# Scores of two attention groups: two products over stacked copies, or three products of 64 rows each

## The chip, the cores and the metric

The kernel runs on one core of a Trainium2 chip. The metric is the device time of one execution in microseconds (us): median 1858.41 us of three runs (1857.59 to 1861.31). The engines are named as in the profile: PE (matrix products), PEld (the loading of a product's stationary operand, which runs beside PE), DVE, ACT, POOL, SP (issues the DMAs).

## The reference

Two layers of a transformer trunk over 512 latent and 256 context tokens of width 1024. The input projection of each layer feeds four head groups in parallel: A (windowed attention, 4 query heads on 2 key heads, with a sink), B (differential attention), C (retention), D (2-D neighbourhood attention, 4 heads). Their outputs go through one output projection, then an MLP. The change touches the scores of A and D alone, per query block of 128 tokens:

```python
# A, per head
s_win  = einsum('bgrnqd,bgnkd->bgrnqk', qb, kw) * scale      # up to 3 key blocks of 128
s_win  = where(valid, s_win, NEG_INF)
s_ctx  = einsum('bgrnqd,bgkd->bgrnqk', qb, k_ctx) * scale    # 256 context keys
prob   = softmax_f32(concatenate([s_win, s_ctx, s_sink], -1))
# D, per head
s      = einsum('bhrjqd,bhrjkwd->bhrjqkw', qg, kg) * scale + bias
s_ctx  = einsum('bhrjqd,bhkd->bhrjqk', qg, k_ctx) * scale
prob   = softmax_f32(concatenate([where(col_valid, s, NEG_INF), s_ctx], -1))
```

A head has 64 channels. Everything is float32; the result of the second layer for the latent tokens is the output.

## The kernel before

Activations lie transposed, channels on the 128 partitions and tokens along the free dimension. Products run on float32r operands, and where float32 accuracy is wanted a value is split into a high part and a low part (`split`): a projection (`gemm`, lines 314 to 328) makes three products per weight tile, high by high (L321), high by low (L322), low by high (L326).

One tile of queries or keys holds two heads of 64 channels, one in partitions 0 to 63 and one in 64 to 127. For A, B, C and D the kernel makes stacked copies of it. `qstack` (L605) makes one tile per head with the high part of that head in one half of the partitions and its low part in the other. `kstack` (L614) makes two tiles per head, one with the high part in both halves and one with the low part in both; the second half is filled by a DMA from the first (`KCOPY`). `qkmm` (L702) then needs two products over all 128 rows for a head: queries by high keys and queries by low keys, which together are all four partial products.

`band_pair` (L737) takes two (block, head) items: in A the two query heads that share a key head, in D two query blocks of one head. The context scores of both items (128 x 256 each) go to the two halves of one PSUM tile `psc`; the window scores of each (128 x 256 at the first and last block, 128 x 384 at the two between, none for context queries) go to a PSUM tile of their own. The tag `ps` has two buffers (`PSB = 2`). DVE adds mask or bias and takes the row maximum while it copies the scores to SBUF (L735, L757), ACT takes the exponential (L763) and scales (L770); then PE transposes the probabilities (L809 in A, L1025 in D) and multiplies by the values (`pvmm`, L713 to L716). The products at L713 and L716 have 64 columns of weights.

`weave` (L106) writes the program: the attention of one unit is mixed with the projections of the next units, by the costs that the generators yield and the totals `CA0` to `CD1`. A scheduler then sets the order on each engine from priorities, readiness and buffers; on PE that order is fixed. `rstd`, `meansq` and `mod_mm` make float32 products with 32 columns of weights, three or four side by side in different column quarters of the array (L244, L266, L350); they are called quarter products below.

Of the kernel before, what the change touches and what calls it, by code (L numbers as in the profile page):

```python
# [12 lines left out]
OP = mybir.AluOpType  # L13
# [5 lines left out]
NT = NX + NC_  # L19
# [3 lines left out]
NEG = -1e30  # L23
# [131 lines left out]
def body(ctx: ExitStack, tc, A):  # L155
    nc = tc.nc
    V, S, G, T, SY = nc.vector, nc.scalar, nc.gpsimd, nc.tensor, nc.sync
# [19 lines left out]
    def pso():  # L177
        return pp.tile([128, 512], F32, name=nm("po"), tag="po", bufs=POB)

    def pss():  # L180
        return pp.tile([128, 512], F32, name=nm("ps"), tag="ps", bufs=PSB)
# [7 lines left out]
    for w in (128, 64, 32):  # L189
        t = cons.tile([128, 32], F32, name=f"gmean{w}")  # L190
# [7 lines left out]
    with tc.tile_pool(name="sp0", bufs=1) as sp0:  # L198
        t = sp0.tile([128, 3, 128], F32, name="spread0")
        V.memset(t, 0.0)  # L200
        for j in range(3):
            r = slice(32 * j, 32 * j + 32)
# [75 lines left out]
    def split(src, hi, lo):  # L278
        S.activation(hi, src, AF.Copy)  # L279
        V.tensor_tensor(lo, src, hi.bitcast(F32), op=OP.subtract)  # L280
# [52 lines left out]
    def u3r(p):  # L333
        return main.tile([128, 768], F32R, name=nm(p), tag="u3", bufs=U3)
# [138 lines left out]
    for L in range(DEPTH):  # L473
        last = L == DEPTH - 1
        nq = NX if last else NT
        lam_init = 0.8 - 0.6 * math.exp(-0.3 * L)
        cl = colc[:, L, :]
        rb = rowb[:, L, :]
# [5 lines left out]
        if L == 0:  # L484
# [38 lines left out]
            h = htiles()  # L523
# [24 lines left out]
        else:  # L548
            xsrc = xd
            h = hnext  # L550
# [6 lines left out]
        GI = {}  # L557
# [26 lines left out]
        def oft(c):  # L584
            of[c] = u3("of")
            return of[c]
# [16 lines left out]
        HALF = (slice(0, 64), slice(64, 128))  # L603
# [10 lines left out]
        def kstack(t, n):  # L614
# [7 lines left out]
                KCOPY(y[b, :n], y[a, :n])  # L622
            return st, lo

        def quarter(i):
            return slice(32 * i, 32 * i + 32)

# [74 lines left out]
        def qkmm(o, q, k, h, qs, ks, keys_first):  # L702

            for i, part in enumerate(k):
                x, y = q[h][:, qs], part[h][:, ks]
                if keys_first:
                    x, y = y, x
                T.matmul(o, lhsT=x, rhs=y, start=(i == 0), stop=(i == 1))

        def pvmm(po, c0, l, vv, hh, t, ph, pl, start, stop):  # L710

            if stop:
                T.matmul(po[0:64, c0:c0 + l], lhsT=vv[:, hh, t, 0:64], rhs=pl, start=False, stop=False)  # L713
            T.matmul(po[:, c0:c0 + l], lhsT=vv[:, hh, t], rhs=ph, start=start, stop=stop)  # L714
            if not stop:
                T.matmul(po[0:64, c0:c0 + l], lhsT=vv[:, hh, t, 0:64], rhs=pl, start=False, stop=False)  # L716
# [16 lines left out]
        def rowmax(dst, src, init, acc):  # L733

            V.tensor_tensor_reduce(dst, src, zcol.to_broadcast([128, src.shape[-1]]), 1.0, init, OP.add, OP.max, acc)  # L735

        def band_pair(items, sinks):  # L737


            sm = smalls()  # L740
            psc = pss()
            res = []
            for i, (n, q, k, h, mask) in enumerate(items):
                qs = slice(128 * n, 128 * n + 128)
                qkmm(psc[:, 256 * i:256 * i + 256], q, k, h, qs, slice(512, 768), False)
            yield 700
            for i, (n, q, k, h, mask) in enumerate(items):
                win = [] if n >= 4 else [t for t in (n - 1, n, n + 1) if 0 <= t < 4]
                w = 128 * len(win)
                P = ptile()  # L750
                rowmax(P[:, w:w + 256], psc[:, 256 * i:256 * i + 256], NEG if sinks is None else sinks[:, i:i + 1], sm[:, i:i + 1])
                if w:
                    qs = slice(128 * n, 128 * n + 128)
                    ks = slice(128 * win[0], 128 * win[0] + w)
                    ps = pss()
                    qkmm(ps[:, :w], q, k, h, qs, ks, False)
                    V.tensor_tensor_reduce(P[:, :w], ps[:, :w], mask, 1.0, sm[:, i:i + 1], OP.add, OP.max, sm[:, 2 + i:3 + i])  # L757
                    yield 450
                res.append((P, win + [4, 5], w))
            ms = sm[:, 2:4] if res[0][2] else sm[:, 0:2]  # L760
            V.tensor_scalar(sm[:, 4:6], ms, -1.0, None, op0=OP.mult)
            for i, (P, _, w) in enumerate(res):
                S.activation(P[:, :w + 256], P[:, :w + 256], AF.Exp, bias=sm[:, 4 + i:5 + i], accum_out=sm[:, 6 + i:7 + i])  # L763
            if sinks is not None:
                V.tensor_tensor(sm[:, 10:12], sm[:, 4:6], sinks, op=OP.add)
                S.activation(sm[:, 10:12], sm[:, 10:12], AF.Exp)
                V.tensor_tensor(sm[:, 6:8], sm[:, 6:8], sm[:, 10:12], op=OP.add)
            V.reciprocal(sm[:, 12:14], sm[:, 6:8])
            for i, (P, _, w) in enumerate(res):
                S.activation(P[:, :w + 256], P[:, :w + 256], AF.Copy, scale=sm[:, 12 + i:13 + i])  # L770
            yield 0
            return [(P, kts) for P, kts, _ in res]

        nblk = 4 if last else 6
        m16 = [(i + 16) % 32 for i in range(32)]
# [6 lines left out]

        def in_a(_):
            tab = ropetab('A')
            k = yield from qk(kstack, 'ak', NT, 2, tab, GI['ak'], m16)
            v = yield from vt('av')
            q = []
            for r in range(2):
                q.append((yield from qk(qstack, f'aq{r}', nq, 2, tab, GI['aq'], m16)))
            return q, k, v  # L790

        def at_a(_, q, k, v):
            vv = v
            amask = grptile()
            SY.dma_start(out=amask[:, 0:384], in_=A['amask'])
            o = [oft(0), oft(1)]
            for n in range(nblk):
                po = pso()
                for g in range(2):
                    am = amask[:, {0: 128}.get(n, 0):{3: 256}.get(n, 384)]  # L800
                    Ps = yield from band_pair([(n, q[r], k, g, am) for r in range(2)],
                                              rb[:, 2 * g:2 * g + 2])
                    kts = Ps[0][1]
                    for i in range(0, len(kts), 2):
                        kk = kts[i:i + 2]
                        pt = pst()
                        for a in range(len(kk)):
                            for r in range(2):
                                T.transpose(pt[:, 256 * a + 128 * r:256 * a + 128 * r + 128],  # L809
                                            Ps[r][0][:, 128 * (i + a):128 * (i + a) + 128], ident)  # L810
                        pth, ptl = ptt()
                        l = 256 * len(kk)
                        split(pt[:, :l], pth[:, :l], ptl[:, :l])
                        for a, t in enumerate(kk):
                            cs = slice(256 * a, 256 * a + 256)
                            pvmm(po, 256 * g, 256, vv, g, t, pth[:, cs], ptl[:, cs], i + a == 0, i + a == len(kts) - 1)
                        yield 540 * len(kk)
                ev = evac_t(po, 512)
                for g in range(2):
                    for r in range(2):  # L820
                        c = 256 * g + 128 * r
                        V.tensor_tensor(o[r][64 * g:64 * g + 64, 128 * n:128 * n + 128], po[0:64, c:c + 128],
                                        ev[:, c:c + 128], op=OP.add)
# [160 lines left out]


        def in_d(u):
            k = yield from qk(kstack, f'dk{u}', NT, 2, None, GI['dk'], None, True)
            v = yield from vt(f'dv{u}', True)
            q = yield from qk(qstack, f'dq{u}', nq, 2, None, GI['dq'], None, True)
            return q, k, v  # L990

        def at_d(u, q, k, v):
            vv = v
            od = oft(6 + u)
            for hh in range(2):
                hd = 2 * u + hh
                rows = slice(64 * hh, 64 * hh + 64)
                bt = grptile()
                SY.dma_start(out=bt[:, 0:896], in_=A['dbias'][L, hd])
                dm = {0: bt[:, 0:256], 1: bt[:, 256:640], 2: bt[:, 256:640], 3: bt[:, 640:896], 4: None, 5: None}  # L1000
                for n2 in range(nblk // 2):
                    Pb = yield from band_pair([(n, q, k, hh, dm[n]) for n in (2 * n2, 2 * n2 + 1)], None)
                    slots = []
                    for t in ([4, 5, 0, 1, 2, 3]):
                        has = [b for b in range(2) if t in Pb[b][1]]
# [83 lines left out]
        for m in range(8):  # L1089
            ps = drain(gemm(wload(A['wout'][L, m], 6, 8), osp, halves(nq)))  # L1090
# [12 lines left out]
        ps = [(pst()[:, :l], s, l) for s, l, _ in parts]  # L1103
# [9 lines left out]
        for Q in range(4):  # L1113
            mid = []
            for f in range(8):
                ps = drain(gemm(wload(A['w1'][L, 8 * Q + f]), h2, [(0, 256), (256, 258)] if last else [(0, 512), (512, 258)]))
# [191 lines left out]
```

## Time and profile before

| what | value |
|---|---|
| median of 3 runs | 1858.41 us |
| the profiled execution, its span | 1859.82 us, 1858.0 us |
| PE, PEld busy | 1816.2 us (98%), 1503.1 us (81%) |
| DVE, ACT busy | 1286.8 us (69%), 958.9 us (52%) |
| granted PE clock, mean | 0.99 |
| score products of A and D on PE | 288 |
| A's scores in layer 0 and 1 | from 79.9 us; around 1155 to 1225 us |
| D's scores in layer 0 and 1 | around 420 to 495 us; to 1454 us |

A row of the timeline gives the start, the time from the first start to the last end, and the instruction; with xN it merges N of the same line. A product's own record is longer than its share of PE, since products follow each other before the one ahead has ended: what one costs is read from the distance between two starts. `128*64` behind the names is rows by columns of the stationary operand, `128x256` what streams through.

### The profile page before, as it was taken

The page shows a single profiled execution, that of the slowest core. Times are in us where ns is not written, and L with a number is a line of the kernel's source. Part 1 is how long each engine was busy: PE and PEld are TensorE (multiplying, and loading weights), DVE is VectorE, ACT ScalarE, POOL GpSimd, SP SyncE. Part 2 cuts the span into 40 slices and gives each one's busy share as a digit, 9 for nine tenths or more (in the row PEclk, how much of TensorE's full clock was granted, in tenths as well). Part 3 has the DMA queues.
Part 4 walks back from the last instruction along what each step waited for, and adds up shares of the span by engine and source line. Part 5 has one row for each costly group of instructions (what it writes and reads, how often), then busy time and mean ns, then how long its engine had stood idle before and what let it go on. Part 6 is the DMA issues. An engine that isn't in the chain of part 4 may idle for free. (4 is left out here: it accounts for less than half of the span.)

```text
span 1858.0 us, 29749 instructions
## 1 busy us (share of the span) xinstructions
PE 1816.2 (98%) x10928; PEld 1503.1 (81%) x10928; DVE 1286.8 (69%) x2985; ACT 958.9 (52%) x1909; POOL 0.2 (0%) x4
## 2 busy tenths in 40 slices
PE   6998999999999999999999999999899999999999
PEld 3787777778868888888888777878677788989897
DVE  6888877788766666666666368897898764545353
ACT  4687656778563213213213356876688663434241
POOL 0000000000000000000000000000000000000000
PEclk9998989999999999999999999999999999999999
DMA  8334334432323343343342353233243223232322
GB/s 303 101 94 127 112 98 131 151 104 67 120 85 108 119 131 113 120 136 109 120 141 91 108 169 102 75 107 86 79 137 100 86 96 97 91 98 95 98 89 94
DMA packets 110418, 208.69 MB, mean 112 GB/s; under 512 B 14272, under 2 KB 20160, under 8 KB 110272
## 3 DMA queue, kind: packets, MB, share of 16 engines
q1 hardware_dynamic: 110272, 206.78, 35.4%
q8 instruction: 86, 1.41, 0.3%
q14 instruction: 60, 0.49, 0.1%
HBM read 182.09 MB, written 5.24 MB: 101 GB/s over the span
## 5 line engine op out<-in xcount | busy, mean ns | idle before, releaser
L279 ACT ACTIVATE wh<-wr 128x512 fp32r<-128x512 f32 (+1 forms) x414 | 253.4, 613 | 620.9 <-PE mm L322 586.1
L321 PE MATMUL mm<-hh,wh 128*128 128x512 f32 (+2 forms) x1680 | 522.6, 330 | 1.3 <-ACT hh L450 1.1
L322 PE MATMUL mm<-hl,wh 128*128 128x512 f32 (+2 forms) x1680 | 518.9, 327 | 0.0
L280 DVE TENSOR_TENSOR wl<-wr,wh 128x512 fp32r<-128x512 f32 (+1 forms) x414 | 275.2, 666 | 208.6 <-ACT wh L279 136.5
L326 PE MATMUL mm<-hh,wl 128*128 128x512 f32 (+2 forms) x1680 | 356.4, 325 | 1.5 <-DVE wl L280 1.5
L321 PEld LDWEIGHTS mm<-hh,wh 128*128 128x128 f32 x1680 | 319.1, 190 | 42.9 <-issue 10.1
L322 PEld LDWEIGHTS mm<-hl,wh 128*128 128x128 f32 x1680 | 319.5, 190 | 28.1 <-issue 3.9
L326 PEld LDWEIGHTS mm<-hh,wl 128*128 128x128 f32 x1680 | 261.4, 189 | 26.7 <-DVE wl L280 1.8
L321 PE MATMUL mm<-mh,wh 128*128 128x512 f32 (+1 forms) x768 | 265.0, 356 | 0.4 <-DVE mh L1128 0.3
L322 PE MATMUL mm<-ml,wh 128*128 128x512 f32 (+1 forms) x768 | 264.2, 355 | 0.0
L326 PE MATMUL mm<-mh,wl 128*128 128x512 f32 (+1 forms) x768 | 181.1, 355 | 0.0
L321 PEld LDWEIGHTS mm<-mh,wh 128*128 128x128 f32 x768 | 144.8, 189 | 24.1 <-ACT wh L279 2.5
L322 PEld LDWEIGHTS mm<-ml,wh 128*128 128x128 f32 x768 | 145.1, 189 | 22.0 <-issue 1.6
L402 DVE SCALAR_TENSOR_TENSOR acc<-wm,silp,acc 128x512 f32<-128x512 f32 x196 | 139.7, 746 | 32.1 <-DMA wm<-in_wmod_dram 31.8
L326 PEld LDWEIGHTS mm<-mh,wl 128*128 128x128 f32 x768 | 131.1, 189 | 24.1 <-issue 4.5
L714 PE MATMUL po<-pth,vv 128*128 128x256 f32 (+2 forms) x328 | 105.9, 328 | 4.2 <-ACT pth L279 3.4
L280 DVE TENSOR_TENSOR ptl<-pt,pth 128x512 fp32r<-128x512 f32 (+3 forms) x148 | 92.1, 630 | 24.9 <-ACT pth L279 22.6
L1139 DVE SCALAR_TENSOR_TENSOR x<-mm,modc,x 128x512 f32<-128x512 f32 (+1 forms) x96 | 63.2, 658 | 64.3 <-PE mm L326 64.3
L279 ACT ACTIVATE pth<-pt 128x512 fp32r<-128x512 f32 (+3 forms) x148 | 79.9, 547 | 34.1 <-PE pt L880 25.2
L714 PEld LDWEIGHTS po<-pth,vv 128*128 128x128 f32 x328 | 62.2, 190 | 25.6 <-ACT pth L279 18.1
L1123 DVE TENSOR_TENSOR zq<-mm,nacc 128x256 f32<-128x256 f32 (+1 forms) x128 | 61.9, 484 | 26.8 <-PE mm L326 25.0
L716 PE MATMUL po<-ptl,vv 128*64 128x256 f32 (+2 forms) x256 | 77.6, 316 | 2.1 <-DVE ptl L280 1.9
(249 smaller groups left out, 2594.9 us busy)
## 6 DMA issues: line engine op xcount, KB each, us to landing
wr<-in_w_dram SPq DMA_DIRECT2D x272, 256.0 KB, 2.6
wm<-in_wmod_dram SPq DMA_DIRECT2D x112, 256.0 KB, 3.0
wr<-in_win_dram SPq DMA_DIRECT2D x96, 256.0 KB, 3.1
wr<-in_wmodh_dram SPq DMA_DIRECT2D x48, 256.0 KB, 3.4
st<-sp SPq DMA_DIRECT2D x96, 96.0 KB, 2.1
w<-in_wmod_dram SPq DMA_DIRECT2D x16, 384.0 KB, 7.2
tx<-in_dd_dram SPq DMA_DIRECT2D x8, 512.0 KB, 3.8
zm<-in_dd_dram SPq DMA_DIRECT2D x16, 256.0 KB, 3.5
```

The lines of the kernel that those rows point to most:

```text
L279: S.activation(hi, src, AF.Copy)
L280: V.tensor_tensor(lo, src, hi.bitcast(F32), op=OP.subtract)
L321: T.matmul(p, lhsT=w[k][0], rhs=act[k][0][:, s:s + l], start=(k == 0), stop=False)
L322: T.matmul(p, lhsT=w[k][0], rhs=act[k][1][:, s:s + l], start=False, stop=False)
L326: T.matmul(p, lhsT=w[k][1], rhs=act[k][0][:, s:s + l], start=False, stop=(k == n - 1))
L402: V.scalar_tensor_tensor(acc[:, v], r, sil[:, k, v:v + 1], acc[:, v], op0=OP.mult, op1=OP.add)
L714: T.matmul(po[:, c0:c0 + l], lhsT=vv[:, hh, t], rhs=ph, start=start, stop=stop)
L716: T.matmul(po[0:64, c0:c0 + l], lhsT=vv[:, hh, t, 0:64], rhs=pl, start=False, stop=False)
L1123: V.tensor_tensor(r[:, s:s + l], p[:, :l], y2[:, s:s + l], op=OP.mult)
L1139: V.scalar_tensor_tensor(xx, p, modc[:, 40 + m, s // 512:s // 512 + 1], xx, op0=OP.mult, op1=OP.add)
```

## The change

For A and D the stacked copies go. `parts2` splits the two-head tile into a high and a low tile, with one ACT and one DVE instruction of 128 partitions. `qkpair` forms the scores of two heads from six products of 64 rows: high by high, high by low, low by high, with the two heads by turns, one in rows 0 to 63 of the array and one in rows 64 to 127. `band_pair` now takes one query block and the two heads of one tile; the context scores of the two heads get a PSUM tile each, the window scores too. In A, the pairs are formed for both query tiles of a block before the values are multiplied; in D, for two blocks, and both heads' bias tables are loaded at the start. C keeps `qstack`, `kstack` and `qkmm`; B keeps its own copies.

```diff
+        def parts2(t, n):
+            st = u3r("qh"), u3r("ql")
+            split(t[:, :n], st[0][:, :n], st[1][:, :n])
+            return st
...
+        def qkpair(outs, qs, ks):
+            for i, (a, b) in enumerate(((0, 0), (0, 1), (1, 0))):
+                for h, (o, q, k) in enumerate(outs):
+                    T.matmul(o, lhsT=q[a][HALF[h], qs], rhs=k[b][HALF[h], ks], start=(i == 0), stop=(i == 2))
...
-        def band_pair(items, sinks):
+        def band_pair(n, items, sinks):
             sm = smalls()
-            psc = pss()
+            psc = [pss(), pss()]
             res = []
-            for i, (n, q, k, h, mask) in enumerate(items):
-                qs = slice(128 * n, 128 * n + 128)
-                qkmm(psc[:, 256 * i:256 * i + 256], q, k, h, qs, slice(512, 768), False)
-            yield 700
...
+            qkpair([(p[:, 0:256], q, k) for p, (q, k, _) in zip(psc, items)], qs, slice(512, 768))
+            yield 360
+            for i, p in enumerate(psc):
                 P = ptile()
-                rowmax(P[:, w:w + 256], psc[:, 256 * i:256 * i + 256], ...)
-                if w:
-                    ps = pss()
-                    qkmm(ps[:, :w], q, k, h, qs, ks, False)
-                    V.tensor_tensor_reduce(P[:, :w], ps[:, :w], mask, ...)
-                    yield 450
+                rowmax(P[:, w:w + 256], p[:, 0:256], ...)
                 res.append((P, win + [4, 5], w))
+            if w:
+                psw = [pss(), pss()]
+                qkpair([(p[:, :w], q, k) for p, (q, k, _) in zip(psw, items)], qs, slice(128 * win[0], 128 * win[0] + w))
+                yield 1.4 * w
+                for i, (p, (_, _, mask)) in enumerate(zip(psw, items)):
+                    V.tensor_tensor_reduce(res[i][0][:, :w], p[:, :w], mask, ...)
...
-            k = yield from qk(kstack, 'ak', NT, 2, tab, GI['ak'], m16)
+            k = yield from qk(parts2, 'ak', NT, 2, tab, GI['ak'], m16)
...
-                q.append((yield from qk(qstack, f'aq{r}', nq, 2, tab, GI['aq'], m16)))
+                q.append((yield from qk(parts2, f'aq{r}', nq, 2, tab, GI['aq'], m16)))
...
+                Pr = []
+                for r in range(2):
+                    Pr.append((yield from band_pair(n, [(q[r], k, am)] * 2, rb[:, r:r + 3:2])))
                 for g in range(2):
-                    Ps = yield from band_pair([(n, q[r], k, g, am) for r in range(2)], rb[:, 2 * g:2 * g + 2])
+                    Ps = [Pr[r][g] for r in range(2)]
```

The order on PE at the start of A in layer 0. Before, `ks`, `kl` and `qs` are the stacked tiles, `mm` a projection that is mixed in:

```order
L321 MATMUL mm_1043<-hh_228,wh_1033 128x512
L708 MATMUL ps_1051<-ks_681,qs_800 128x256
L322 MATMUL mm_1043<-hl_229,wh_1033 128x512
L708 MATMUL ps_1051<-kl_683,qs_800 128x256
L321 MATMUL mm_1043<-hh_230,wh_1033 128x512
```

And now, for the context scores of block 0, `ps_1044` the head in rows 0 to 63, `ps_1045` the one in rows 64 to 127:

```order
L721 MATMUL ps_1044<-qh_681,qh_792 128x256
L321 MATMUL mm_1034<-hh_230,wh_1024 128x512
L721 MATMUL ps_1045<-qh_681,qh_792 128x256
L322 MATMUL mm_1034<-hl_231,wh_1030 128x512
L721 MATMUL ps_1044<-ql_682,qh_792 128x256
L326 MATMUL mm_1034<-hh_224,wl_1025 128x512
L721 MATMUL ps_1045<-ql_682,qh_792 128x256
L326 MATMUL mm_1034<-hh_226,wl_1025 128x512
```

Two products over 128 rows, a projection's product between, have become six of 64 rows for two heads, and a projection's product over 128 rows stands between each two of them.

A little later in A, layer 0, the context scores of block 0 for the second query tile (`ps_1064`, `ps_1065`: the two halves of the rows) and the first window scores (`ps_1076`), now:

```order
L721 MATMUL ps_1064<-qh_681,qh_887 128x256
L721 MATMUL ps_1064<-ql_682,qh_887 128x256
L721 MATMUL ps_1064<-qh_681,ql_888 128x256
L322 MATMUL mm_1034<-hl_233,wh_1030 128x512
L321 MATMUL mm_1034<-hh_234,wh_1030 128x512
L322 MATMUL mm_1034<-hl_235,wh_1030 128x512
L321 MATMUL mm_1034<-hh_236,wh_1030 128x512
L322 MATMUL mm_1034<-hl_237,wh_1030 128x512
L721 MATMUL ps_1065<-qh_681,qh_887 128x256
L721 MATMUL ps_1065<-ql_682,qh_887 128x256
L721 MATMUL ps_1065<-qh_681,ql_888 128x256
L721 MATMUL ps_1076<-qh_681,qh_887 128x256
```

Here the three products of one head stand together and those of the other head come five projection products later: the scheduler has not kept the turns in which `qkpair` writes them.

## Rows read from the trace of the kernel before

**Rows 1.** The page, busy time, share of the span and instructions of each engine
```profile
PE 1816.2 (98%) x10928; PEld 1503.1 (81%) x10928; DVE 1286.8 (69%) x2985; ACT 958.9 (52%) x1909; POOL 0.2 (0%) x4
```

**Rows 2.** Windows with A's, D's scores: length; busy PE, PEld, DVE, ACT, POOL; clock
```profile
79.00:150.00 71.00, 69.41 (x470) 58.44 (x469) 57.52 (x191) 57.76 (x134) 0.00 (x0) 0.99 0.33 95
420.00:495.00 75.00, 72.71 (x474) 61.86 (x473) 58.67 (x178) 61.88 (x141) 0.00 (x0) 1.00 0.20 64
1155.00:1225.00 70.00, 69.93 (x448) 59.28 (x448) 61.25 (x201) 59.42 (x130) 0.00 (x0) 1.00 0.28 76
1414.00:1475.00 61.00, 60.57 (x360) 49.37 (x359) 48.43 (x141) 50.04 (x110) 0.00 (x0) 1.00 0.24 80
```

**Rows 3.** Groups on PE by form: the score products of A and D
```profile
L708 PE MATMUL ps<-ks,qs 128*128 128x256 f32 x112 | 31.7, 298 | 0.0
L708 PE MATMUL ps<-kl,qs 128*128 128x256 f32 x112 | 30.3, 284 | 0.0
L708 PE MATMUL ps<-ks,qs 128*128 128x384 f32 x32 | 11.7, 367 | 0.0
L708 PE MATMUL ps<-kl,qs 128*128 128x384 f32 x32 | 10.9, 340 | 0.0
```

**Rows 4.** Timeline of PE from 341.2 us: start, us, line, product
```profile
341.23 0.28 PE L716 MATMUL po<-ptl,vv 128*64 128x256 f32 x1
341.35 0.62 PE L326 MATMUL mm<-hh,wl 128*128 128x512 f32 x2
341.81 0.28 PE L321 MATMUL mm<-hh,wh 128*128 128x256 f32 x1
341.93 0.28 PE L322 MATMUL mm<-hl,wh 128*128 128x256 f32 x1
342.04 0.28 PE L321 MATMUL mm<-hh,wh 128*128 128x256 f32 x1
```

**Rows 5.** Timeline of PE from 78.9 us, quarter products between full ones
```profile
78.94 0.50 PE L321 MATMUL mm<-hh,wh 128*128 128x512 f32 x1
79.39 0.62 PE L244 MATMUL pt<-zq,gmean 128*32 128x256 f32 x2
79.94 0.39 PE L708 MATMUL ps<-ks,qs 128*128 128x256 f32 x1
80.16 0.28 PE L708 MATMUL ps<-kl,qs 128*128 128x256 f32 x1
80.28 0.40 PE L322 MATMUL mm<-hl,wh 128*128 128x512 f32 x1
```

**Rows 6.** Timeline of PEld in the same stretch
```profile
78.93 0.19 PEld L321 LDWEIGHTS mm<-hh,wh 128*128 128x128 f32 x1 [0.41 <-issue]
79.39 0.14 PEld L244 LDWEIGHTS pt<-zq,gmean 128*32 128x32 f32 x2 [0.27 <-ACT zq L659]
79.94 0.19 PEld L708 LDWEIGHTS ps<-ks,qs 128*128 128x128 f32 x1 [0.41 <-issue]
80.04 0.19 PEld L708 LDWEIGHTS ps<-kl,qs 128*128 128x128 f32 x1
80.17 0.19 PEld L322 LDWEIGHTS mm<-hl,wh 128*128 128x128 f32 x1
```

**Rows 7.** Timeline of PE at 346.3 us, eight quarter products
```profile
346.27 0.64 PE L350 MATMUL mm<-wr,silp 128*32 128x256 f32 x8
```

**Rows 8.** Lines L619, L621, L610, L611, L645: count, ns min/median/max, span
```profile
L619 ACT ACTIVATE ks<-zq x20: 830/842/847, 66.1 to 1408.5; 64x768 fp32r<-64x768 f32 x20
...
L621 DVE TENSOR_TENSOR kl<-zq,ks x20: 941/952/957, 67.4 to 1409.4; 64x768 fp32r<-64x768 f32 x20
...
L610 ACT ACTIVATE qs<-zq x24: 617/731/846, 76.7 to 1435.3; 64x768 fp32r<-64x768 f32 x12, 64x512 fp32r<-64x512 f32 x12
...
L611 DVE TENSOR_TENSOR qs<-zq,qs x24: 684/819/955, 78.3 to 1436.0; 64x768 fp32r<-64x768 f32 x12, 64x512 fp32r<-64x512 f32 x12
...
L645 SPq DMA_DIRECT2D ks<-ks x20: 461/472/720, 67.0 to 1409.4; - x20
```

**Rows 9.** Lines L735 and L757 on DVE: count, ns min/median/max, span
```profile
L735 DVE CUSTOM_DVE_ANT_0 P<-ps,zcol x120: 395/418/425, 162.2 to 1452.7; 128x256 f32<-128x256 f32 x120
L757 DVE CUSTOM_DVE_ANT_0 P<-ps,gp,sm x64: 471/542/619, 95.2 to 1454.5; 128x256 f32<-128x256 f32 x32, 128x384 f32<-128x384 f32 x32
```

More of the change, by code (lines that the diff above doesn't have):

```diff
@@ L735, in rowmax @@
             V.tensor_tensor_reduce(dst, src, zcol.to_broadcast([128, src.shape[-1]]), 1.0, init, OP.add, OP.max, acc)
-        def band_pair(items, sinks):
+        def band_pair(n, items, sinks):
             sm = smalls()
-            psc = pss()
+            psc = [pss(), pss()]
             res = []
-            for i, (n, q, k, h, mask) in enumerate(items):
-                qs = slice(128 * n, 128 * n + 128)
-                qkmm(psc[:, 256 * i:256 * i + 256], q, k, h, qs, slice(512, 768), False)
-            yield 700
-            for i, (n, q, k, h, mask) in enumerate(items):
-                win = [] if n >= 4 else [t for t in (n - 1, n, n + 1) if 0 <= t < 4]
-                w = 128 * len(win)
-                P = ptile()
-                rowmax(P[:, w:w + 256], psc[:, 256 * i:256 * i + 256], NEG if sinks is None else sinks[:, i:i + 1], sm[:, i:i + 1])
-                if w:
-                    qs = slice(128 * n, 128 * n + 128)
-                    ks = slice(128 * win[0], 128 * win[0] + w)
-                    ps = pss()
-                    qkmm(ps[:, :w], q, k, h, qs, ks, False)
-                    V.tensor_tensor_reduce(P[:, :w], ps[:, :w], mask, 1.0, sm[:, i:i + 1], OP.add, OP.max, sm[:, 2 + i:3 + i])
-                    yield 450
-                res.append((P, win + [4, 5], w))
+            qs = slice(128 * n, 128 * n + 128)
+            win = [] if n >= 4 else [t for t in (n - 1, n, n + 1) if 0 <= t < 4]
+            w = 128 * len(win)
+            qkpair([(p[:, 0:256], q, k) for p, (q, k, _) in zip(psc, items)], qs, slice(512, 768))
+            yield 360
+            for i, p in enumerate(psc):
+                P = ptile()
+                rowmax(P[:, w:w + 256], p[:, 0:256], NEG if sinks is None else sinks[:, i:i + 1], sm[:, i:i + 1])
+                res.append((P, win + [4, 5], w))
+            if w:
[3 more added lines that the diff above has]
+                for i, (p, (_, _, mask)) in enumerate(zip(psw, items)):
+                    V.tensor_tensor_reduce(res[i][0][:, :w], p[:, :w], mask, 1.0, sm[:, i:i + 1], OP.add, OP.max, sm[:, 2 + i:3 + i])
             ms = sm[:, 2:4] if res[0][2] else sm[:, 0:2]
@@ L798, in at_a @@
                 po = pso()
+                am = amask[:, {0: 128}.get(n, 0):{3: 256}.get(n, 384)]
+                Pr = []
+                for r in range(2):
+                    Pr.append((yield from band_pair(n, [(q[r], k, am)] * 2, rb[:, r:r + 3:2])))
                 for g in range(2):
-                    am = amask[:, {0: 128}.get(n, 0):{3: 256}.get(n, 384)]
-                    Ps = yield from band_pair([(n, q[r], k, g, am) for r in range(2)],
-                                              rb[:, 2 * g:2 * g + 2])
+                    Ps = [Pr[r][g] for r in range(2)]
                     kts = Ps[0][1]
@@ L986, in in_d @@
         def in_d(u):
-            k = yield from qk(kstack, f'dk{u}', NT, 2, None, GI['dk'], None, True)
+            k = yield from qk(parts2, f'dk{u}', NT, 2, None, GI['dk'], None, True)
             v = yield from vt(f'dv{u}', True)
-            q = yield from qk(qstack, f'dq{u}', nq, 2, None, GI['dq'], None, True)
+            q = yield from qk(parts2, f'dq{u}', nq, 2, None, GI['dq'], None, True)
             return q, k, v
@@ L994, in at_d @@
             od = oft(6 + u)
+            dm = []
             for hh in range(2):
-                hd = 2 * u + hh
-                rows = slice(64 * hh, 64 * hh + 64)
                 bt = grptile()
[L999 to L1002, printed above, removed]
+                SY.dma_start(out=bt[:, 0:896], in_=A['dbias'][L, 2 * u + hh])
+                dm.append({0: bt[:, 0:256], 1: bt[:, 256:640], 2: bt[:, 256:640], 3: bt[:, 640:896], 4: None, 5: None})
+            for n2 in range(nblk // 2):
+                Pn = []
+                for n in (2 * n2, 2 * n2 + 1):
+                    Pn.append((yield from band_pair(n, [(q, k, dm[hh][n]) for hh in range(2)], None)))
+                for hh in range(2):
+                    rows = slice(64 * hh, 64 * hh + 64)
+                    Pb = [Pn[i][hh] for i in range(2)]
                     slots = []
```

## The prediction

> **What bounds the kernel now.** I read the page's busy times first. PE is busy for 98% of the span, DVE for 69%, ACT for 52% [rows 1]. A share over the whole run may hide a stage with another limit, so I then looked at the four windows that hold the scores of A and D in the two layers. PE is busy 69.41 of 71, 72.71 of 75, 69.93 of 70 and 60.57 of 61 us there, at a clock of 0.99 to 1.00; DVE and ACT follow with 78 to 88% [rows 2]. So PE sets the time where the change acts, and what PE must do more or less goes to the end nearly one for one. Around these windows stand PE's projections and the MLP, so little later absorbs it. A busy share of 98% also holds the tails of products that overlap. The price of one is therefore its distance to the next start, not its record.
>
> **What is removed from PE.** 112 + 112 score products that stream 256 columns and 32 + 32 of 384 [rows 3]. In a run of 256-column products the starts are 0.11 to 0.12 us apart (341.81, 341.93, 342.04 [rows 4]), and the two 512-column products at 341.35 end 0.62 later with one record of 0.39, so they start 0.23 apart. For 384 I take the middle, 0.175. That makes 224 x 0.118 + 64 x 0.175 = 26.4 + 11.2 = 37.6 us.
>
> **What is added to PE.** Three products for a head in place of two: 336 of 256 columns and 96 of 384. A product costs by its streamed columns, and half the rows save none of these. One after the other they are 336 x 0.118 + 96 x 0.175 = 39.6 + 16.8 = 56.4 us, 18.8 more than before. If two heads in different halves of the rows run at the same time, the six of a pair cost as three, 28.2 us in all and 9.4 less than before; but only where they stand beside each other in PE's order. I counted the whole order of the changed program. The 432 products stand in 178 stretches with other products between; 76 of these stretches hold a single product, and only 68 times can two neighbours of different halves be paired (52 of 256 columns, 16 of 384). The two pieces of the new order above show both patterns. So overlap gives back at most 52 x 0.118 + 16 x 0.175 = 8.9 us, and the products alone cost +9.9 (with overlap) to +18.8 us (without). No row of the trace has a product of 64 rows. Side by side work is seen only with quarter products in different columns: eight of them take 0.64 us with records of about 0.4 [rows 7], four at a time. I take overlap, +9.9, and keep both ends.
>
> **What a change of array shape costs.** This is the largest term. When PE goes from full products to quarter products and back, it pays. L321 at 78.94 has a record of 0.50, not 0.39, because its weights are loaded at 78.93, with it and not ahead of it [rows 5, 6]: 0.11 laid bare. The quarter product after it starts 0.45 later where 0.23 would be the pace; without the 0.11 that leaves 0.11 in which the array empties. Back again, the second of the two quarter products at 79.39 starts at 79.63 (0.62 less a record of 0.38), the full one at 79.94: 0.31, against 0.24 between quarter rounds, so 0.07; and L708 again has 0.39 in place of 0.28, with its load at 79.94, so 0.11. From the second full product on, loads run ahead (80.04 for the product at 80.16). One excursion into another shape whose weights have 128 columns as here is thus 0.11 + 0.11 + 0.07 + 0.11 = 0.40 us. Against this stands L716: 64 columns of weights, float32r, and its neighbour L326 starts 0.12 later, an ordinary distance [rows 4]. So not every smaller product pays. Which of the two a product of 64 rows follows, the trace can't say. The bounds of this term are 178 x 0 = 0 and 178 x 0.40 = 71 us; a value between is 178 x 0.18 = 32 us (emptying alone, loads ahead). I take the upper one, since two heads in the halves of the rows write two result tiles and split the array as the quarters do, while I read L716 as a full product with columns left out. 23 of the changes have a quarter product on their other side, which paid 0.09 there before as well: -2. So +69.
>
> The Trainium skill, page TensorEngine Tiling (Array Packing), section Key Properties, says that a change of tiling mode, not only of the tile, drains the array. By that rule the time is the forecast's, without it the sum is +9.9 and not +79 us before the relief below. The quarter products here agree with it, L716 doesn't.
>
> **What goes on other engines.** `parts2` replaces 6 uses of `kstack` and 8 of `qstack`. On DVE each use loses one of two instructions: 6 x 0.95 + 4 x 0.95 + 4 x 0.69 = 12.3 us; ACT 6 x 0.84 + 4 x 0.84 + 4 x 0.62 = 10.9 us; SP loses 24 DMAs of 0.47, 11.3 us [rows 8]. PE does other products meanwhile, so this frees only what PE waited for in the windows: 1.59 + 2.29 + 0.07 + 0.43 = 4.4 us by rows [rows 2], some more in gaps that records cover. I take -6, between 0 and -12.
>
> **The added waits.** A pair now needs both `ps` buffers for its context scores, then both again for its window scores, 144 takings in place of 104. The first product of the next group stands at the head of PE's fixed queue until DVE has taken the maximum, 0.42 to 0.61 us for a tile [rows 9]; behind it wait all projections. Before, the same wait stood at 104 places, and other products in the order covered it. The second piece of the new order shows five of them, 5 x 0.23 us, between the two halves. I cost it at 0; without cover it is 40 x 0.5 = 20 us. D loads both bias tables at the start, so d1's second table waits for d0's end; projections lie beside it: 0.
>
> **The sum.** +9.9 + 69 - 6 = +73 us. The profiled execution has a span of 1858.0 and 1859.82 in all, 1.4 above the median of 1858.41; from the median I get 1931, and say 1930.
>
> **The rivals.**
> - No drain, no overlap: 64 rows behave as L716 does, like a full product with rows left out. For it: same operand type, no price seen. Then 18.8 - 6 gives 1871; with the added waits up to 1885.
> - No drain, but overlap. 1858.4 + 9.9 - 6 = 1862. For it: quarter products of different columns run together [rows 7]. Against it: each change around them had its price. The Trainium skill, page TensorE: Matmul & The Clock Gate, Part 3 (Packing small matmuls), has products in different row groups run concurrently. By that rule alone this rival's time holds, at best; no run here shows it yet.
> - The array empties, but the weights of a half are loaded ahead: 9.9 + 30 - 6 gives 1892.
> - Faster: in the four windows DVE and ACT, 78 to 88% busy, set PE's pace behind its overlapping records, and the 12.3 us that DVE loses come off whole. This decides once they outweigh the +9.9 of the products, without drains. With everything on its side, 1858.4 + 9.9 - 18 gives 1850. Against it: PE's idle time there is 4.4 us in sum.
>
> **How the numbers follow.** Drain in full 0.55 (1930, own range 1905 to 1945: fewer changes paid where PE waits anyway, or no overlap and some added wait), no drain and no overlap 0.20 (1871), emptying alone 0.07 (1892), overlap without drain 0.12 (1862), faster 0.06 (1850). Ends that leave about one in ten out on each side: 1862 and 1945. 0.2% is 3.7 us, about what a measurement of this kernel tells from no change. Of the overlap case about a third falls within it or below: faster 0.07, same 0.06, slower 0.87.
>
> **What would show it.** In the changed profile, a score product alone between projections (first piece of the new order) shows the term of 69: if its weights are loaded with it and not ahead, its record is 0.11 longer, and the starts around it are 0.2 and more further apart than 0.118 and 0.23, it is right. If the loads run ahead and distances are plain, it is wrong, and the time lies at 1862 to 1885. Overlap is shown by two neighbours of different halves that start within some 0.02 us. The four windows should grow together by some 73 us, the MLP not at all. Waits of L721 on DVE's maxima would show the added-wait term.

## The result and the profile after

The changed kernel takes 1935.99 us (median of 4 runs, 1932.23 to 1940.96), the kernel before beside it 1859.62 us. The ratio is 1.0417, with a 95% interval from 1.0401 to 1.0433: 76.4 us slower. The profiled execution of after took 1940.96 us with a span of 1939.2, 81.2 above the span of before, at a mean granted clock of 0.984; the other three runs had 0.987 to 0.989. So some 5 of the 81 us are this execution's own.

First the page of after: busy time of each engine.

```profile
PE 1894.0 (98%) x11072; PEld 1527.2 (79%) x11072; DVE 1279.9 (66%) x2971; ACT 953.8 (49%) x1895; POOL 0.2 (0%) x4
```

PE has 144 products more than in [rows 1] and is 77.8 us longer busy; DVE and ACT are 6.9 and 5.1 us less busy (time with two records at once counts once). PE's idle time is 45.2 us (1939.2 - 1894.0), before 41.8.

Then where the time lies. The span was cut at the first and the last score product of A and D in each layer. Before (stretch: length; busy PE, PEld, DVE, ACT, POOL; clock, DMA share, GB/s):

```profile
79.90:145.40 65.50, 65.42 (x447) 55.54 (x446) 52.52 (x175) 52.53 (x118) 0.00 (x0) 1.00 0.30 85
145.40:419.00 273.60, 262.45 (x1555) 201.70 (x1554) 223.35 (x571) 184.33 (x399) 0.00 (x0) 0.96 0.42 123
419.00:477.20 58.20, 56.22 (x368) 47.79 (x368) 48.21 (x151) 50.77 (x114) 0.00 (x0) 1.00 0.22 68
477.20:1148.60 671.40, 669.58 (x3888) 560.44 (x3887) 439.08 (x787) 234.84 (x420) 0.00 (x0) 1.00 0.38 120
1148.60:1203.50 54.90, 54.90 (x353) 47.28 (x353) 47.35 (x151) 44.30 (x97) 0.00 (x0) 1.00 0.27 72
...
1406.60:1454.20 47.60, 47.29 (x286) 39.11 (x286) 42.29 (x129) 41.41 (x90) 0.00 (x0) 1.00 0.28 88
```

and after:

```profile
80.00:179.20 99.20, 99.20 (x494) 69.13 (x493) 57.92 (x191) 58.91 (x132) 0.00 (x0) 0.93 0.20 56
179.20:462.50 283.30, 264.32 (x1541) 199.06 (x1539) 217.43 (x550) 175.82 (x377) 0.00 (x0) 0.95 0.38 114
462.50:534.70 72.20, 71.70 (x412) 51.30 (x412) 48.11 (x154) 53.09 (x117) 0.00 (x0) 1.00 0.16 51
534.70:1206.20 671.50, 669.74 (x3890) 560.67 (x3888) 437.47 (x781) 231.79 (x417) 0.00 (x0) 1.00 0.37 118
1206.20:1273.20 67.00, 66.94 (x373) 48.62 (x372) 47.99 (x149) 44.07 (x94) 0.00 (x0) 1.00 0.21 60
...
1473.50:1531.70 58.20, 57.22 (x289) 38.46 (x288) 39.12 (x121) 39.40 (x85) 0.00 (x0) 0.97 0.17 54
```

The four score windows grew by 33.7, 14.0, 12.1 and 10.6 us, 70.4 together. The long stretch with the MLP between D of layer 0 and A of layer 1 is the same (671.40 and 671.50). B and C of layer 0, between A and D, took 9.7 more, those of layer 1 2.8 less, and what follows D of layer 1 3.7 more. In A of layer 0 the clock fell from 1.00 to 0.93.

Next the timeline of PE in A of layer 0, where 64-row products and projections alternate (start, us, product):

```profile
95.25 0.38 PE L721 MATMUL ps<-qh,qh 64*128 64x256 f32 x1
95.56 0.50 PE L322 MATMUL mm<-hl,wh 128*128 128x512 f32 x1
95.99 0.38 PE L721 MATMUL ps<-ql,qh 64*128 64x256 f32 x1
96.30 0.50 PE L326 MATMUL mm<-hh,wl 128*128 128x512 f32 x1
96.73 0.38 PE L721 MATMUL ps<-ql,qh 64*128 64x256 f32 x1
```

and the loading of the weights just there:

```profile
96.30 0.19 PEld L326 LDWEIGHTS mm<-hh,wl 128*128 128x128 f32 x1
96.73 0.18 PEld L721 LDWEIGHTS ps<-ql,qh 64*128 64x128 f32 x1 [0.24 <-issue]
97.04 0.19 PEld L326 LDWEIGHTS mm<-hh,wl 128*128 128x128 f32 x1
```

Every load starts with its product (96.30, 96.73), never ahead of it; in this trace that holds at all 178 changes to 64 rows and at all 178 back. The records are 0.38 and 0.50 instead of 0.28 and 0.39, as at a quarter product [rows 5, 6]. A projection and a score take 0.74 us together (95.25 to 95.99) where the paces of 0.23 and 0.118 make 0.35. So each excursion loses 0.39 here.

Over the whole span, the loads of the score products wait mostly for no engine. This view of L721 counts the idle time ahead of its instructions:

```profile
its engine sat idle before it (us, times) until:
  issue: 25.4, 100
  DVE sm L770: 5.4, 14
  DVE sm L748: 2.9, 10
```

"issue", 100 times, is idle time of PEld in which the load waited for no engine, as the 0.24 at 96.73; an exposed load that follows the one before it without idle time is not in this count (the 128-row version below has 3.3 us, 8 times). L748 and L770 are DVE's maxima, the added waits: 8.3 us in all, where the maxima (L735, L757) held up L708 for 0.6 us before.

Where two heads do stand side by side, the timeline merges the two rows (x2), and the two together take 0.39 us, what one takes alone:

```profile
101.12 0.40 PE L322 MATMUL mm<-hl,wh 128*128 128x512 f32 x1
101.45 0.39 PE L721 MATMUL ps<-qh,qh 64*128 64x256 f32 x2
101.67 0.29 PE L721 MATMUL ps<-ql,qh 64*128 64x256 f32 x2
101.79 0.28 PE L721 MATMUL ps<-qh,ql 64*128 64x256 f32 x2
102.00 0.50 PE L321 MATMUL mm<-hh,wh 128*128 128x512 f32 x1
```

Six products take 0.55 us from the first to the next projection. Behind the first two the loads run ahead, and the pace is 0.12 for two. The two of a pair start 0.01 us apart here; in the whole trace 76 neighbours start less than 0.02 us apart.

### The profile page after: what moved, and what is told of

Read it like the earlier page. It is cut to its first block, busy times and chain, and to the rows that moved or that the text cites. A ratio compares the mean times of both kernels' runs of the same rounds, so it can differ in the third digit from the quotient of the medians.

```text
span 1939.2 us, 29965 instructions
## 1 busy us (share of the span) xinstructions
PE 1894.0 (98%) x11072; PEld 1527.2 (79%) x11072; DVE 1279.9 (66%) x2971; ACT 953.8 (49%) x1895; POOL 0.2 (0%) x4
## 5 line engine op out<-in xcount | busy, mean ns | idle before, releaser
L326 PE MATMUL mm<-hh,wl 128*128 128x512 f32 (+2 forms) x1680 | 365.8, 329 | 2.1 <-DVE wl L280 2.1
L280 DVE TENSOR_TENSOR ptl<-pt,pth 128x512 fp32r<-128x512 f32 (+2 forms) x148 | 91.7, 629 | 31.5 <-ACT pth L279 30.0
L279 ACT ACTIVATE pth<-pt 128x512 fp32r<-128x512 f32 (+2 forms) x148 | 79.9, 547 | 58.5 <-PE pt L893 21.3
```

Of the source, the lines that this page charges most:

```text
L326: T.matmul(p, lhsT=w[k][1], rhs=act[k][0][:, s:s + l], start=False, stop=(k == n - 1))
```

## The experiments

Theory: the loss is 178 changes of the array's shape at 0.3 to 0.4 us, and side by side the 64-row products are nearly free. Rivals: the third product itself, the added waits on `ps`, or the work on DVE and ACT.

**The same products over 128 rows.** The pairs, their turns and the PSUM tiles stay as changed; the keys of the other head are zeros in a tile of full height.

```diff
-                    T.matmul(o, lhsT=q[a][HALF[h], qs], rhs=k[b][HALF[h], ks], start=(i == 0), stop=(i == 2))
+                    T.matmul(o, lhsT=q[a][:, qs], rhs=k[b][h][:, ks], start=(i == 0), stop=(i == 2))
...
+                S.activation(x[:, :n], t[:, :n], AF.Copy, scale=mcol[:, h:h + 1])
+                V.scalar_tensor_tensor(y[:, :n], t[:, :n], mcol[:, h:h + 1], x[:, :n].bitcast(F32), op0=OP.mult, op1=OP.subtract)
```

> The same three products per head, the same pairs, PSUM tiles and order rules as the changed kernel, but each over all 128 rows: the keys of the other head are zeroed (two ACT and two DVE instructions per key tile instead of one each, no copies by DMA). No change of array shape and no overlap. If the shape changes cost the time (178 x 0.40 = 71 us), they go, and 336 x 0.118 + 96 x 0.175 - 37.6 = 18.8 us of products stay: 1859.6 + 18.8, less up to 6 us: 1872 to 1880. If the number of products with the waits for the two ps buffers is the cause, it stays near 1936.

Measured: 1887.11 us, ratio 1.0157 (1.0141 to 1.0172). Of the 76 us, 48.9 go when only the height of the operands changes, though three products per head, all pairs and all waits for `ps` stay, and what overlap there was is lost with it. The time is 7 to 15 us above what I expected. Two windows of this run's profile (its slowest execution, 1890.82), A of layer 0 and what follows up to D:

```profile
80.00:154.70 74.70, 74.63 (x479) 61.78 (x478) 54.28 (x183) 56.01 (x129) 0.00 (x0) 1.00 0.26 71
154.70:442.70 288.00, 269.04 (x1567) 204.78 (x1566) 221.29 (x559) 179.27 (x387) 0.00 (x0) 0.93 0.38 113
```

A has its clock back, but B and C take 288.0 us at a clock of 0.93, 14.4 more than before, with 19.0 us of PE idle (before 11.2). That is a second effect; the totals below test it.

**Fewer excursions, the same products.** First the six products of a pair are kept in their written order on PE, at a higher priority; the scheduler then still puts others between in part: 144 stretches, 150 pairs of different halves.

```diff
+            with tc.high_priority(offset=1000), tc.manual_schedule(engines={mybir.EngineType.PE}):
+                for i, (a, b) in enumerate(((0, 0), (0, 1), (1, 0))):
+                    for h in (1, 0):
...
```

> The changed kernel, with the six products of a pair kept in the order in which they are written and at a higher priority. The order on PE then has 144 stretches (178 in the changed kernel) and 150 neighbours in different halves (68). With shape changes at 0.40 us a stretch and overlap at 0.13 us a pair: 18.8 - 19.5 + 57.6 - 2 = +55, 1914. With shape changes and no overlap: +74, 1934. If neither counts: 1936 as before.

Measured: 1920.67 us (1916.37 to 1928.41), ratio 1.0346 (1.0316 to 1.0376). 15 us less than the changed kernel, between the two values of the expectation and nearer to the one with overlap; its clock was no better, 0.978 to 0.984. Second, a full product of 2 columns ahead of each group takes the wait for both PSUM tiles, so that the six start at once: 78 stretches, all 216 pairs side by side.

```diff
+                T.matmul(outs[1][0][:, 0:2], lhsT=outs[1][1][0][:, qs], rhs=outs[1][2][0][:, 0:2], start=True, stop=True)
```

> As the run before it, with one product of two columns over all 128 rows ahead of each pair, which takes the second PSUM tile, so that the six then follow each other: 78 stretches, 216 neighbours in different halves, 72 small products of some 0.11 us more. With shape changes at 0.40 and overlap at 0.13: 18.8 - 28.2 + 31 + 8 = +30, 1889. Without overlap: +58, 1917. If PE's waits for the ps buffers are what costs, it gets slower than the changed kernel, since the first product now waits for both buffers: over 1936.

Measured: 1892.81 us, ratio 1.018 (1.0164 to 1.0195), within 4 us of the theory, 24 below the value without overlap and 43 below the rival of `ps`. The 43 us against the changed kernel are not the stretches alone: 100 excursions fewer are 38 us at the price measured below, 216 pairs side by side instead of 68 take the products from +9.9 to -9.4, 19 us, and the small products cost some 8. That makes 49.

**One excursion by itself.** To the kernel before, 128 products of 256 columns were added in the MLP, one between two projection products, their results unused: over 128 rows, over rows 0 to 63, and over both halves side by side. Nothing is left out.

```diff
...
+                    if step in (0, 6):
+                        for r0 in (0,):
+                            dm = pss()
+                            r = slice(r0, r0 + 64)
+                            tc.keep_in_program_order(T.matmul(dm[:, 0:256], lhsT=h2[0][0][r, 0:128], rhs=h2[1][0][r, 0:256], start=True, stop=True))
...
```

(shown for rows 0 to 63)

> The kernel before, with 128 more products of 256 columns in the MLPs, two in each product group of L321, over all 128 rows, float32r, result unused. PE waits for nothing there. 128 x 0.118 = 15 us: 1875. All theories agree; it is the yardstick.

> The same 128 products over rows 0 to 63 only. If a change of array shape costs 0.40 us, 128 x (0.118 + 0.40) = 66 us: 1926. If 64 rows behave like full products, as the products with 64 columns do: 1875 as its yardstick. If the array empties but weights are loaded ahead: 128 x (0.118 + 0.18) = 38 us: 1898.

> 128 pairs of products, one over rows 0 to 63 and one over rows 64 to 127, side by side, into two PSUM tiles. With overlap a pair costs as one product: within 3 us of the run with one half, 1926 to 1929. Without overlap 15 us more: 1941.

Measured: 1874.96 us (+16.5 over before's 1858.47; ratio 1.0085, 1.007 to 1.01), 1923.0 (+64.5; 1.0344, 1.0326 to 1.0361) and 1926.95 (+68.5; 1.0365, 1.035 to 1.0381), each within 3 us of what a price of 0.40 and full overlap let expect. A full product costs 16.5/128 = 0.129 us. Half the rows cost (64.5 - 16.5)/128 = 0.375 us more, with no wait and no other work in play. The second half costs 4.0/128 = 0.03 us. The records of the added products, over 128 rows and over 64 (count, ns min/median/max, span):

```profile
L1129 PE MATMUL ps<-hh,hh x128: 275/283/384, 543.5 to 1820.3; 128*128 128x256 f32 x128
...
L1129 PE MATMUL ps<-hh,hh x128: 378/381/384, 545.5 to 1873.4; 64*128 64x256 f32 x128
```

With 64 rows not one of the 128 has the plain record of 283 ns. Around one pair (rows of PE's timeline):

```profile
551.24 0.28 PE L322 MATMUL mm<-hl,wh 128*128 128x258 f32 x1
551.45 0.39 PE L1129 MATMUL ps<-hh,hh 64*128 64x256 f32 x2
551.77 0.38 PE L321 MATMUL mm<-hh,wh 128*128 128x258 f32 x1
551.99 0.28 PE L322 MATMUL mm<-hl,wh 128*128 128x258 f32 x1
```

The starts are 0.21, 0.32 and 0.22 apart, where three plain ones would be 0.12: 0.09 on the way in, 0.11 of the 64-row products' load and 0.09 on the way out, 0.10 of load after. The exposed loads show in the records; that the array empties in the two times 0.09 is my reading of what the loads leave over.

**The totals of the weave.** The changed yields (360 and 1.4 per column for a pair) no longer fit the totals, by which attention and projections are mixed. Scaled, first with the 128-row products:

```diff
-CA0 = 39.9
+CA0 = 32.1
...
-CD0 = 18.9
+CD0 = 15.7
-CA1 = 40.8
+CA1 = 32.8
...
-CD1 = 11
+CD1 = 9.2
```

> The run with full rows (1887), with the four totals that weave divides by (CA0, CD0, CA1, CD1) scaled to what the new generators yield: 32.1, 15.7, 32.8, 9.2 in place of 39.9, 18.9, 40.8, 11. In that run layer 0 took some 14 us more between the end of A and the start of D, where nothing was changed. If that comes from totals that the attention of A no longer reaches, so that projections are handed out late, it goes: 1873 to 1878. If it comes from the two ps buffers or from anything else, it stays at 1887.

Measured: 1869.67 us, ratio 1.0062 (1.0046 to 1.0077), 17.4 less than without the scaling and a little better than expected. The stretch from A to D of layer 0:

```profile
156.40:416.90 260.50, 253.12 (x1529) 193.74 (x1528) 215.47 (x556) 177.08 (x384) 0.00 (x0) 0.99 0.41 121
```

27.5 us shorter, with PE idle for 7.4 instead of 19.0 us and the clock at 0.99 instead of 0.93 ((0.99 - 0.93) x 288 is 17 us of full speed). So the second effect is in this stretch: PE waits there for DVE and ACT (at B's scores and transposes, at the products by the values and at norms), and runs at the lower clock for part of it. The same on the version with 78 stretches:

> The run with one stretch for a pair (1893), with the totals scaled as in the run with full rows and totals. If the totals are worth the same 17 us here: 1876. The products by themselves (18.8 - 28.2), 78 x 0.375 for the shape and 72 small products at 0.11 make +28, 1887, if the totals were worth nothing here beyond what the sum leaves.

Measured: 1873.98 us, ratio 1.0082 (1.0067 to 1.0097), 19 less and 2 below what I expected. And on the changed kernel itself:

> The changed kernel with the four totals of the weave scaled to the scores' new yields (CA0 32.1, CD0 15.7, CA1 32.8, CD1 9.2) and nothing else. The new order has 204 stretches of 64-row products instead of 178 and 56 pairs of different halves instead of 68, so by 0.375 us for each excursion and 0.118 for each pair it should lose 26 x 0.375 + 12 x 0.118 = 9.8 + 1.4 = 11 us. Theory (the unpredicted rest of the change is the granted clock in A and B of layer 0, which the totals move, as they did with the 128-row products: 33 us less at half speed, 17 us less time): the mean clock rises from 0.984-0.989 to 0.992 or more, 10 to 17 us come back, the time is 1930 to 1937 us. Rival (the rest lies in the excursions and not in the clock): 1936 + 11 = 1947 us with the clock of before, or 1936 + 11 and a clock that rises without effect.

Measured: 1935.62 us (1934.58 to 1942.75), ratio 1.0421 (1.0396 to 1.0445): no change against 1935.99. The time lies in the theory's range, but not by its means: the clock is 0.983 to 0.988, not 0.992. A to D of layer 0 did get 22.1 us shorter; A of layer 0 stays at 0.93:

```profile
79.30:182.20 102.90, 102.73 (x516) 70.81 (x514) 58.31 (x191) 60.67 (x138) 0.00 (x0) 0.93 0.23 63
182.20:443.40 261.20, 254.93 (x1520) 193.56 (x1519) 214.75 (x551) 173.95 (x374) 0.00 (x0) 0.98 0.42 120
```

PE's idle time over the span fell from 45.2 to 32.5 us; 26 excursions more at 0.375 are 9.8 us, which takes most of that back. Twelve of them lie in D of layer 0 (58 stretches, before the scaling 46), which takes 84.0 us at a clock of 0.96 instead of 72.2 at 1.00. The lower clock of A in layer 0 does not come from the totals: with the 128-row products A is at 1.00 with either totals. Nor do 64-row products alone bring it. The version kept at 144 stretches has the same 432 products, and this is its A in layer 0:

```profile
77.90:153.50 75.60, 75.60 (x469) 54.40 (x469) 55.65 (x186) 56.55 (x128) 0.00 (x0) 1.00 0.23 64
```

Its three other score windows are at 1.00 too, and so is A with 78 stretches. Only the two orders with most changes of shape (178 and 204 stretches) show the lower clock there, each in the one execution that was profiled.

The last run and the 128-row version with the same totals also make the cleanest pair: products, PSUM tiles and totals are the same, only the height of the operands differs, with the masking of the keys and the order that the scheduler then sets. They lie 1935.62 - 1869.67 = 66 us apart; 204 x 0.375 less 56 x 0.118 for the pairs gives 70.

**The same rule on the kernel before.** The quarter products change the array's shape 135 times before. Their rounds were kept together, the stacked copies stay: 95 stretches with a high priority, 114 without.

```diff
-        for j in range(3):
+        with tc.high_priority(offset=1000), tc.manual_schedule(engines={mybir.EngineType.PE}):
+            for j in (2, 0, 1):
...
-        for k in range(8):
-            mod_mm(p[:, 0:256], k, w[k])
+        with tc.high_priority(offset=1000), tc.manual_schedule(engines={mybir.EngineType.PE}):
+            for k in range(7, -1, -1):
+                mod_mm(p[:, 0:256], k, w[k])
```

> The kernel before, with the float32 products of 32 columns (L244, L266, L350) kept together and the last-ready one first, at a higher priority: 95 stretches of them in the order in place of 135. If each change of shape and back costs about 0.3 us: 40 x 0.31 = 12 us less, 1846. If the change of shape costs nothing there: no difference. If PE now waits for the last operand, it is slower.

> As the run before it without the higher priority: 114 stretches. 21 x 0.31 = 6 to 7 us less, 1852; no difference if the change of shape costs nothing.

Measured: 1836.91 us, ratio 0.9883 (0.9868 to 0.9898), and 1850.31, ratio 0.9956 (0.9944 to 0.9969). The first is the fastest version in this study, 21.6 us below before, where I expected 12. Part of the rest is the packing itself: 592 neighbouring quarter products start less than 0.02 us apart in this trace, 520 in that of before, and 72 x 0.119 is 9 us. With 40 excursions at 0.31 to 0.375 us, 12 to 15, that makes 21 to 24. PE's idle time rose by 4 us, so a few us stay unexplained.

Both together, this grouping and the 78 stretches with their totals:

> The run above with the quarter products grouped too (21.6 us in the kernel before): 1855. If it is under 1837, products of 64 rows are worth having once stretches are few; if over, the stacked copies stay the better way.

Measured: 1851.03 us, ratio 0.9954 (0.9937 to 0.997), 4 below the 1855 expected. It is 14 above the grouping alone: as far as these versions go, the stacked copies stay the better way to form the scores.

## Why the prediction was right

The forecast was 1930 us by a drain in full; 1935.99 was measured, and the profile and the runs show most of the steps named.

- **Bound by PE, windows grow, MLP not.** Right: 70.4 us in the four windows against 73 foretold, 0.1 in the stretch of the MLP.
- **178 changes of shape at 0.40 us.** Right, a little high: 0.375 in the MLP, 0.39 in the first rows above, with the load exposed as foretold. 178 x 0.375 = 67, where the forecast had 71. The choice between quarter products [rows 5] and L716 [rows 4] was the right one; no row of before could settle it, and the chance of 0.55 says so. By the Trainium skill, page TensorEngine Tiling (Array Packing), section Key Properties, a change of tiling mode drains the array; the runs here agree for 64 rows (0.375 us) and not for L716.
- **Overlap, products +9.9.** Right: 76 neighbours start together (68 were counted), and the second half costs 0.03 us. That the overlap alone would give 1862 fell to the price of the excursions.
- **Emptying alone (1892), no drain (1871), faster by DVE and ACT (1850).** Fell: loads are exposed at all 178 changes, the excursion has its price without any other cause, and the work taken from DVE and ACT, 12.3 and 10.9 us by the sums of their instructions as foretold, left none of the four windows shorter.
- **The added waits at 0.** Nearer to 0 than to the 20 without cover, but not nothing: L748 and L770 hold up the score products, nearly always at their load, for 5.4 + 2.9 us in all, 24 times, and PE itself shows 0.7 us of it. In the 128-row version, which has the same products and tiles, the waits for maxima come to 2.9 us, so they are 5 of the 49 us at most.
- **Missed: the granted clock.** The forecast had no term for it. Its mean fell from 0.990 to 0.984: 0.010 x 1858 = 18.6 us of full speed were missing before, 0.016 x 1939.2 = 31.0 after, 12 more, if PE is busy throughout; PE's idle time adds 3. With the terms as measured, 67 - 2 + 9.9 + 12 + 3 = 90 against 81.2. In the three other executions (0.987 to 0.989) the clock term is smaller, 3 to 7 us by the same sum.
- **Not isolated: the relief of -6.** In the four windows as cut above, PE's idle time fell from 2.4 to 1.5 us; [rows 2], which reach past the scores, had 4.4. What lies in gaps that records cover can be summed from the traces: the distance of every start on PE to the next, less the pace (0.119, 0.175 and 0.23 us for 256, 384 and 512 columns). Around the 64-row products this excess is 74 us, 5 of them at the lower clock and the waits for `ps` among them, so the excursions were not cheaper than those in the MLP. Everywhere else it changed by -4: -17 at full clock, +13 at the lower. The products by their paces, quarter products included, add 11, and 74 - 4 + 11 is the 81. The -17 holds the relief, but also waits that now stand ahead of 64-row products; no run separates the two. In the 128-row version with its totals scaled, where no product has 64 rows, the same sum at full clock is -6.

So the mechanism held, and the forecast came within 6 us partly by luck: the clock term that it lacked and gaps elsewhere that shrank by more than the -6 largely cancel.

## What to carry to other kernels

Count the changes of the array's shape in PE's final order, not in the source: each excursion from full products to 64 rows and back costs 0.375 us here, as much as three 256-column products. Packing pays where a whole packed group stands in one stretch, and a scheduler that fills waits with other products takes it apart; price the groups by stretches and by the pairs that really stand side by side (from 178 stretches and 68 pairs to 78 and 216 gave 43 us, from 135 to 95 stretches of quarter products 21.6). After a change of the yields of a mix, look at the stage behind it too: rescaled totals were worth 17 and 19 us in two versions here and nothing in the third, where they brought more excursions.

## What the runs showed of the hardware

A product of 64 rows and 128 columns between full ones costs 0.375 us beyond its pace, with its own load and that of the full product behind it exposed. One of 128 rows and 64 columns (L713, L716) costs nothing beyond its pace: in the whole trace of before the median distance is 0.118 us from a full 256-column product to it (126 times) and 0.119 us from it to a full one (176 times; [rows 4] shows one). Both kinds were float32r. A pair in the two halves of the rows costs 0.03 us more than one.

The clock can fall during the alternation itself, with PE busy throughout. A of layer 0 in the changed kernel:

```profile
136.72 0.38 PE L721 MATMUL ps<-qh,ql 64*128 64x256 f32 x1
137.03 0.39 PE L322 MATMUL mm<-hl,wh 128*128 128x256 f32 x1
137.35 0.38 PE L721 MATMUL ps<-qh,ql 64*128 64x256 f32 x1
...
139.25 0.41 PE L321 MATMUL mm<-hh,wh 128*128 128x256 f32 x1
139.59 0.58 PE L721 MATMUL ps<-qh,qh 64*128 64x256 f32 x1
139.97 0.41 PE L721 MATMUL ps<-ql,qh 64*128 64x256 f32 x1
```

Up to 137.35 the starts are 0.31 apart; from 138 us on a product's record is 0.41 to 0.58. The window just behind (columns as in the windows above):

```profile
140.00:150.00 10.00, 10.00 (x39) 8.32 (x39) 4.68 (x14) 1.58 (x3) 0.00 (x0) 0.50 0.00 0
```

The granted clock is 0.50, the lower of its two levels of 1.2 and 2.4 GHz, while PE is busy for 10.00 of 10.00 us. What went before is the alternation, without idle time but with the 0.09 us at each change that I read as emptying. What exactly lowers the clock no run here isolates: the 128 lone products of 64 rows in the MLP left the mean at 0.988 to 0.991, as before, and in the order with 144 stretches the clock of A stayed at 1.00.
